# Column mean of an 8192 x 8192 matrix: plain two-row-group loads and three unsummed row groups left to TensorE

## The chip, the core and the metric

The kernel runs on one core of one Trainium2 chip. A core has TensorE (PE, matrix products), VectorE (DVE), ScalarE (ACT), GpSimd (POOL), SyncE (SP, here only an issuer of transfers) and 16 DMA engines that move data between the chip's memory and the core's own memory, SBUF. TensorE writes its results to a small accumulating memory, PSUM, from which ScalarE or VectorE must copy them before they can be stored. The metric is device time in microseconds (us) of one execution. SBUF has 128 partitions; a tile is written "partitions x elements".

## The reference

```python
def setup_inputs():
    return {"x": np.random.randn(8192, 8192).astype(np.float32)}

def reference(x):
    return np.mean(x, axis=0)
```

The input is 8192 rows of 8192 float32 numbers, 268.4 MB. The output is one row of 8192 numbers, the mean of each column. Every input byte is read once and takes part in one addition.

## The kernel before, in words

**Tiling.** The rows are cut into G = 64 row groups of 128 rows, one row for each partition; a group is 4 MB. The columns are counted in 16 blocks of F = 512, and W = 128 is a quarter of a block. The buffer `bufs` holds six whole row groups: slots 0 to 3 are a ring for loads, slot 4 is `both` (the sum of the two groups of a load), and slot 5 is `acc`, the running sum over row groups. VectorE adds row groups into `acc`, so that `acc` becomes 128 partial sums for each column. Summing over the 128 partitions is left to TensorE: a matmul with `ones` (128 x 32, every value 1/8192) as weights gives the sum over partitions. Each matmul makes 32 equal output rows, so four of them, at four column tiles of the array (`tile_position=(0, 32 * q)`), fill the 128 partitions of one PSUM tile with four different stretches of columns. A float32 matmul of the code is two MATMUL records in the profile.

**Loads.** All loads go out from SyncE in the order of the program (`load`, L73). A load waits for the add that last read its slot, and each second one also for two loads eight places back. First come 512 KB of row group 60 (blocks 14 and 15) into a separate tile `early`, then groups 0 to 3 as one load of 16 MB, groups 4 and 5 as one load, and 1.25 MB of group 63 (blocks 9 to 13) into `early`. After that groups 6 to 55 come two at a time (`load_rows`, L89), groups 56 to 59 one at a time, group 60 without the two blocks that came early, 61 and 62 whole, and the rest of group 63 in four pieces: blocks 4 to 7, 0 to 3, 14 to 15, and 8.

**VectorE.** `add` (L94) makes one addition. For a pair of groups there are two: `both` = first + second, then `acc` += `both`; the ring slot is free for the next load after the first of them. A no-op on ScalarE or GpSimd waits for the load and for the addition ahead together, and the addition waits for that no-op. Groups 56 to 60 are added to `acc` singly. Of group 60 only blocks 0 to 13 are added, of group 61 only blocks 7 to 15.

**GpSimd** adds the two early pieces into `acc` while VectorE and the loads go on (L129), and at the end three blocks of group 62 (L148).

**TensorE** runs 63 matmuls at the end, in the order of the list `sums` (L155 to L180): blocks of `acc` and of groups 61, 62 and 63, ordered by when each becomes final, into the PSUM tiles `bank0`, `bank1`, `wide`, `two` and `last`. The list is executed in that order, whatever is ready.

**Results.** ScalarE copies four of the PSUM tiles into the no longer used slot `both` (L198), VectorE copies `last` into `tail` (L214). Five stores (L201) go out, from SyncE and from ScalarE. SyncE then waits for every load and store, and the program ends.

The functions that the change touches:

Of the kernel before, what the change touches and what calls it, by code (L numbers as in the profile page):

```python
# [9 lines left out]
def kernel(  # L10
# [35 lines left out]
    sync = mybir.DependencyInfo(mybir.DependencyClass.Sync, mybir.DependencyReason.DATA)  # L46

    sb = ctx.enter_context(tc.tile_pool(name="sb", bufs=1))
    psp = ctx.enter_context(tc.tile_pool(name="psum", bufs=1, space=bass.MemoryType.PSUM))

    bufs = sb.tile([P, U, N], f32, name="bufs")
    both = bufs[:, U - 2, :]
    acc = bufs[:, U - 1, :]
    ones = sb.tile([P, 32], f32, name="ones")
    early = sb.tile([P, 7 * F], f32, name="early")
    tail = sb.tile([P, W], f32, name="tail")
    warm = sb.tile([P, 32], f32, name="warm")
    nc.gpsimd.memset(ones[:], 1.0 / M)  # L58
    ready = sb.tile([P, 1], f32, name="ready")
    tc.keep_in_program_order(  # L60
        nc.gpsimd.tensor_add(out=ready[:], in0=ones[:, 0:1], in1=ones[:, 1:2]))  # L61
    banks = [psp.tile([P, F], f32, name=f"bank{b}") for b in range(2)]
    wide = psp.tile([P, 2 * F], f32, name="wide")
    two = psp.tile([P, 2 * W], f32, name="two")
    last = psp.tile([P, W], f32, name="last")

    loads = []

    def landed(*inss):

        nop = tc.keep_in_program_order(nc.sync.nop()).ins
        for o in inss:
            tc.add_manual_dep(nop, o.name, sync, reason="SyncE waits")  # L73

    def load(dst, src):
        ins = tc.keep_in_program_order(nc.sync.dma_start(out=dst, in_=src)).ins  # L76
# [12 lines left out]
    def load_rows(g, u, n):  # L89
        return load(bufs[:, u:u + n, :], rows(g, n).rearrange("(p j) c -> p j c", j=n))  # L90

    adds, joins = [], {}

    def add(dst, a, b, dmas):  # L94

        ins = nc.vector.tensor_add(out=dst, in0=a, in1=b).ins  # L96
# [10 lines left out]
        tc.declare_no_dep(ins, group="early", reason="the no-op waited, or the add behind it")  # L107
        tc.add_to_no_dep_group("adds", ins)
        adds.append(ins)

    load(early[:, 5 * F:], rows(G - 4)[:, 14 * F:])
    first, second = load_rows(0, 0, 4), load_rows(4, 4, 2)
    load(early[:, :5 * F], rows(G - 1)[:, 9 * F:14 * F])
    add(bufs[:, 2:4, :], bufs[:, 2:4, :], bufs[:, 0:2, :], [first])
    add(bufs[:, 4:6, :], bufs[:, 4:6, :], bufs[:, 2:4, :], [second])
    add(acc, acc, both, [])
    tc.keep_in_program_order(nc.scalar.copy(out=warm[:], in_=ones[:]))  # L117
    ahead = []
    g = 6
    while g < G - 8:  # L120
        u = (g + 2) % 4
        dma = load_rows(g, u, 2)
        add(both, bufs[:, u, :], bufs[:, u + 1, :], [dma])
        add(acc, acc, both, ahead)
        ahead = []
        if g in (24, 32):
            lo, hi = (0, 4) if g == 24 else (4, 7)
            cols = slice((9 + lo) * F, (9 + hi) * F)
            ins = tc.keep_in_program_order(nc.gpsimd.tensor_add(  # L129
                out=acc[:, cols], in0=acc[:, cols], in1=early[:, lo * F:hi * F])).ins  # L130
            tc.add_to_no_dep_group("early", ins)
            ahead = [ins]
        g += 2

    while g < G - 4:
        row = bufs[:, (g + 2) % 4, :]
        add(acc, acc, row, [load(row, rows(g))])
        g += 1
    for lo, hi, loaded in [(0, 14, 14), (7, 16, 16)]:
        row = bufs[:, (g + 2) % 4, :]  # L140
        dma = load(row[:, :loaded * F], rows(g)[:, :loaded * F])
        cols = slice(lo * F, hi * F)
        add(acc[:, cols], acc[:, cols], row[:, cols], [dma])
        g += 1
    r61, r62, r63 = [bufs[:, (g + 1 + j) % 4, :] for j in range(3)]
    load(r62, rows(g))
    for cols in [slice(14 * F, 16 * F), slice(8 * F, 9 * F)]:
        joined = tc.keep_in_program_order(nc.gpsimd.tensor_add(  # L148
            out=acc[:, cols], in0=acc[:, cols], in1=r62[:, cols])).ins
    g += 1  # L150
    for lo, hi in [(4, 8), (0, 4), (14, 16), (8, 9)]:
        load(r63[:, lo * F:hi * F], rows(g)[:, lo * F:hi * F])

    sums = []

    def blocks(row, lo, hi):
        for i in range(lo, hi):
            sums.append((banks[i // 4], i % 4, 0, row[:, i * F:(i + 1) * F]))

    def spread(dst, row, lo, hi, part=slice(None)):  # L160
        n = (hi - lo) * W
        for c in range(0, n, F)[part]:
            for q in range(4):
                at = lo * F + q * n + c
                sums.append((dst, q, c, row[:, at:at + min(F, n - c)]))

    blocks(acc, 2, 5)
    blocks(acc, 0, 2)
    blocks(r61, 0, 7)
    blocks(acc, 5, 8)  # L170
    blocks(r62, 0, 8)
    spread(wide, acc, 9, 14, slice(1))
    blocks(r63, 4, 8)
    spread(wide, r62, 9, 14, slice(1))
    for row in (acc, r62):
        spread(wide, row, 9, 14, slice(1, 2))
    spread(two, acc, 14, 16)
    blocks(r63, 0, 4)
    spread(last, acc, 8, 9)
    spread(two, r63, 14, 16)  # L180
    spread(last, r63, 8, 9)
    for n, (dst, q, c, cols) in enumerate(sums):
        summed = tc.keep_in_program_order(nc.tensor.matmul(  # L183
            out=dst[32 * q:32 * q + 32, c:c + cols.shape[1]],
            lhsT=ones[:],
            rhs=cols,
            start=all((d is dst, k, at) != (True, q, c) for d, k, at, _ in sums[:n]),
            stop=all((d is dst, k, at) != (True, q, c) for d, k, at, _ in sums[n + 1:]),
            tile_position=(0, 32 * q),
            skip_group_check=True,  # L190
        )).ins

    res = both[:, :2 * F].rearrange("p (b c) -> p b c", b=2)
    res5 = both[:, 2 * F:2 * F + 5 * W]
    res2 = both[:, 4 * F:4 * F + 2 * W]

    def copy(dst, src):
        return tc.keep_in_program_order(nc.scalar.copy(out=dst, in_=src)).ins  # L198

    def store(engine, dst, src, *then):  # L200
        ins = tc.keep_in_program_order(engine.dma_start(out=dst, in_=src)).ins  # L201
        for o in then:
            tc.add_manual_dep(ins, o.name, sync, reason="follows that load")
        return ins

    def part(lo, hi):
        return out[lo * F:hi * F].rearrange("(q c) -> q c", q=4)

    copy(res[:, 1, :], banks[1][:])
    s1 = store(nc.scalar, part(4, 8), res[0:P:32, 1, :], loads[-4])  # L210
    copy(res5, wide[:, :5 * W])
    copy(res[:, 0, :], banks[0][:])
    copied = copy(res2, two[:])
    ended = nc.vector.tensor_copy(out=tail[:], in_=last[:]).ins  # L214
    landed(*joins.values())
    s5 = store(nc.sync, part(9, 14), res5[0:P:32, :], *loads[-7:-3])
    s0 = store(nc.sync, part(0, 4), res[0:P:32, 0, :])
    s2 = store(nc.scalar, part(14, 16), res2[0:P:32, :])
    store(nc.sync, part(8, 9), tail[0:P:32, :])
    landed(loads[-2], joined)  # L220
    landed(loads[-1], copied)
    landed(s0, s5)
    landed(s1, summed)
    landed(s2, ended)
# [32 lines left out]
```

## Time and profile before

| | |
|---|---|
| median of 3 runs | 628.5 us (628.38 to 628.59) |
| the profiled execution, first to last instruction (span) | 626.4 us |
| VectorE busy | 529.3 us, 85% of the span |
| TensorE busy | 13.3 us, 2%, all of it at the end |
| share of the 16 DMA engines' time taken by packets of the load queue | 99.3% |
| data rate over the span | 429 GB/s |

Of the profiled execution the page gives the span and not a total of its own; the median of the timed runs stands 2.1 us above that span, which is what lies around the first and last instruction. Where sums below are made, they are made inside the span, and the difference is put on the median.

The profile's views used here are the page itself (busy times, DMA queues, groups of instructions), the chain of waits (followed back from the last instruction: at each step what released it), and the timeline (instructions of each engine in order of time). In the chain, a piece named DMA is time in which the chain ran through a load. In the timeline PEld is the loading of weights for TensorE, PE the matmuls themselves; SPq and ACTq are the issuing of a transfer by SyncE or ScalarE.

### The profile page before, as it was taken

The numbers are of one execution on the slowest core, as the hardware profiler recorded it, in microseconds if no ns is written. First come the engines' busy times: TensorE is split into PE (matmuls) and PEld (weight loads), VectorE is DVE, ScalarE is ACT, GpSimd is POOL, SyncE is SP. The second block draws the span as 40 slices with busy tenths as digits, with TensorE's granted clock in tenths as the row PEclk, the third lists the DMA queues.
The fourth block names the chain that finished last, engine by engine and source line by source line (L and its number), as shares of the span: only waits on it lengthen the run. The fifth ranks groups of instructions, "written<-read, shape, count | busy, mean of one in ns | idle before, by whom it ended". The sixth has DMA issues, their size and how long they took to land.

```text
span 626.4 us, 484 instructions
## 1 busy us (share of the span) xinstructions
PE 13.3 (2%) x126; PEld 4.0 (1%) x126; DVE 529.3 (85%) x60; ACT 3.7 (1%) x6; POOL 12.0 (2%) x10
## 2 busy tenths in 40 slices
PE   0000000000000000000000000000000000000008
PEld 0000000000000000000000000000000000000002
DVE  0028999998888998889998899888898888999992
ACT  0000000000000000000000000000000000000001
POOL 0000000000000000020000200000000000000002
PEclk9999999999999999999999999999999999999999
DMA  8999999999999999999999999999999999999997
GB/s 372 465 402 428 459 410 460 402 469 402 469 402 469 402 469 402 469 402 469 402 465 406 439 431 427 444 410 460 402 469 402 469 402 469 402 435 435 419 435 305
DMA packets 5930, 268.50 MB, mean 429 GB/s; under 512 B 660, under 2 KB 668, under 8 KB 1064
## 3 DMA queue, kind: packets, MB, share of 16 engines
q1 hardware_dynamic: 5912, 268.46, 99.3%
q8 instruction: 1, 0.02, 0.0%
q10 hardware_dynamic: 16, 0.01, 0.0%
q14 instruction: 1, 0.01, 0.0%
HBM read 268.44 MB, written 0.03 MB: 429 GB/s over the span
## 4 chain that ended last, share of the span: by engine, by line
DMA 59%; DVE 30%; another core or an unknown queue 10%; issue 0%; SPq 0%; ACTq 0%; PE 0%; POOL 0%; POOLq 0%
DMA bufs<-in_x_dram 59%; DVE bufs L96 30%; SPq L76 0%; ACTq L99 0%; PE last L183 0%; DVE tail L214 0%; POOL ready L61 0%; POOL ones L58 0%; POOLq L99 0%; POOLq L241 0%
## 5 line engine op out<-in xcount | busy, mean ns | idle before, releaser
L96 DVE TENSOR_TENSOR bufs<-bufs 128x8192 f32<-128x8192 f32 (+3 forms) x59 | 529.0, 8966 | 85.9 <-DMA bufs<-in_x_dram 43.0
L183 PE MATMUL bank<-bufs,ones 128*32 128x512 f32 x62 | 10.0, 716 | 610.3 <-DVE bufs L96 610.0
L129 POOL TENSOR_TENSOR bufs<-bufs,early 128x2048 f32<-128x2048 f32 (+1 forms) x2 | 7.9, 3954 | 348.5 <-DVE bufs L96 348.5
L148 POOL TENSOR_TENSOR bufs<-bufs 128x1024 f32<-128x1024 f32 (+1 forms) x2 | 3.6, 1824 | 258.9 <-DMA bufs<-in_x_dram 258.9
L214 DVE COPY tail<-last 128x128 f32<-128x128 f32 x1 | 0.3, 291 | 8.8 <-PE last L183 8.8
L183 PEld LDWEIGHTS bank<-bufs,ones 128*32 128x32 f32 x62 | 2.2, 121 | 616.4 <-issue 614.5
L198 ACT COPY bufs<-bank 128x512 f32<-128x512 f32 x2 | 1.2, 586 | 617.9 <-PE bank L183 617.9
L183 PE MATMUL wide<-bufs,ones 128*32 128x512 f32 (+1 forms) x32 | 2.5, 432 | 0.0
L117 ACT ACT_TABLE_LOAD x1 | 1.3, 1283 | 0.7 <-PEq L241 0.7
L183 PE MATMUL two<-bufs,ones 128*32 128x256 f32 x16 | 1.2, 380 | 0.0
L183 PEld LDWEIGHTS wide<-bufs,ones 128*32 128x32 f32 x32 | 1.0, 110 | 1.8 <-issue 1.8
L183 PE MATMUL last<-bufs,ones 128*32 128x128 f32 x16 | 0.8, 279 | 0.1
L198 ACT COPY bufs<-wide 128x640 f32<-128x640 f32 x1 | 0.7, 692 | 1.1 <-PE wide L183 1.1
L183 PEld LDWEIGHTS last<-bufs,ones 128*32 128x32 f32 x16 | 0.4, 109 | 1.2 <-issue 0.6
L183 PEld LDWEIGHTS two<-bufs,ones 128*32 128x32 f32 x16 | 0.4, 109 | 0.1
L198 ACT COPY bufs<-two 128x256 f32<-128x256 f32 x1 | 0.4, 372 | 0.1
L117 ACT COPY warm<-ones 128x32 f32<-128x32 f32 x1 | 0.2, 217 | 0.0
L61 POOL TENSOR_TENSOR ready<-ones 128x1 f32<-128x1 f32 x1 | 0.2, 193 | 0.1
L58 POOL MEMSET ones<- 128x32 f32 x1 | 0.1, 125 | 0.3 <-POOLq L241 0.3
L241 POOL MEMSET const-float32-0.0<- 128x1 f32 x1 | 0.1, 98 | 0.2 <-issue 0.2
L241 POOL MEMSET const-bfloat16-1.0<- 128x1 bf16 x1 | 0.1, 102 | 0.0
L241 POOL MEMSET const-uint8-127<- 128x1 uint8 x1 | 0.1, 102 | 0.0
(1 smaller groups left out, 0.1 us busy)
## 6 DMA issues: line engine op xcount, KB each, us to landing
bufs<-in_x_dram SPq DMA_DIRECT2D x6, 4096.0 KB, 20.4
bufs<-in_x_dram SPq DMA_DIRECT2D x1, 3584.0 KB
bufs<-in_x_dram SPq DMA_DIRECT2D x2, 1024.0 KB, 18.7
early<-in_x_dram SPq DMA_DIRECT2D x1, 1280.0 KB
early<-in_x_dram SPq DMA_DIRECT2D x1, 512.0 KB
bufs<-in_x_dram SPq DMA_DIRECT2D x1, 512.0 KB, 19.4
bufs<-in_x_dram SPq DMA_DIRECT2D x27, 29.9
bufs<-in_x_dram SPq DMA_DIRECT2D x1, 256.0 KB, 19.7
```

What stands on the lines that cost most here:

```text
L58: nc.gpsimd.memset(ones[:], 1.0 / M)
L61: nc.gpsimd.tensor_add(out=ready[:], in0=ones[:, 0:1], in1=ones[:, 1:2]))
L96: ins = nc.vector.tensor_add(out=dst, in0=a, in1=b).ins
L117: tc.keep_in_program_order(nc.scalar.copy(out=warm[:], in_=ones[:]))
L129: ins = tc.keep_in_program_order(nc.gpsimd.tensor_add(out=acc[:, cols], in0=acc[:, cols], in1=early[:, lo * F:hi * F])).ins
L148: joined = tc.keep_in_program_order(nc.gpsimd.tensor_add(out=acc[:, cols], in0=acc[:, cols], in1=r62[:, cols])).ins
L183: summed = tc.keep_in_program_order(nc.tensor.matmul(out=dst[32 * q:32 * q + 32, c:c + cols.shape[1]], lhsT=ones[:], rhs=cols, start=all(( ...
L198: return tc.keep_in_program_order(nc.scalar.copy(out=dst, in_=src)).ins
L214: ended = nc.vector.tensor_copy(out=tail[:], in_=last[:]).ins
L241: nc = _bacc.Bacc("TRN2", target_bir_lowering=False, num_devices=1)
```

## The change

All loads but the last four now have two row groups each: 31 of them, for groups 0 to 61. The two early loads, the load of four groups, and the single loads are gone. Group 62 is one load; group 63 is three: blocks 0 to 10, 11 to 14, and 15.

VectorE makes 60 additions of a whole row group: one for groups 0 and 1 (straight into `acc`), two for each of the 29 pairs 2 to 59, and one for group 60. Groups 61, 62 and 63 are added by nobody; TensorE takes them whole. GpSimd adds nothing any more.

TensorE runs 80 matmuls: for each of `acc`, group 61, 62 and 63, in this order, the same 20 over all 16 blocks. The PSUM tiles are four banks (blocks 0 to 3, 4 to 7, 8 to 10, 11 to 14) and `last` (block 15).

The results get SBUF tiles of their own. ScalarE copies banks 0, 2 and 3, VectorE bank 1 and `last`. SyncE issues the stores of banks 0, 1, 2 and of `last`; ScalarE issues one, that of bank 3.

```diff
-    early = sb.tile([P, 7 * F], f32, name="early")
+    res = [sb.tile([P, w], f32, name=f"res{i}") for i, w in enumerate((F, F, 3 * W, F))]
...
-    load(early[:, 5 * F:], rows(G - 4)[:, 14 * F:])
-    first, second = load_rows(0, 0, 4), load_rows(4, 4, 2)
-    load(early[:, :5 * F], rows(G - 1)[:, 9 * F:14 * F])
-    add(bufs[:, 2:4, :], bufs[:, 2:4, :], bufs[:, 0:2, :], [first])
-    add(bufs[:, 4:6, :], bufs[:, 4:6, :], bufs[:, 2:4, :], [second])
-    add(acc, acc, both, [])
+    def pair(g):
+        u = g % 4
+        dma = load(bufs[:, u:u + 2, :], rows(g, 2).rearrange("(p j) c -> p j c", j=2))
+        return bufs[:, u, :], bufs[:, u + 1, :], dma
+
+    a, b, dma = pair(0)
+    add(acc, a, b, [dma])
...
-    while g < G - 8:
-        u = (g + 2) % 4
-        dma = load_rows(g, u, 2)
-        add(both, bufs[:, u, :], bufs[:, u + 1, :], [dma])
-        add(acc, acc, both, ahead)
...
-    while g < G - 4:
-        row = bufs[:, (g + 2) % 4, :]
-        add(acc, acc, row, [load(row, rows(g))])
-        g += 1
-    for lo, hi, loaded in [(0, 14, 14), (7, 16, 16)]:
...
-    for lo, hi in [(4, 8), (0, 4), (14, 16), (8, 9)]:
-        load(r63[:, lo * F:hi * F], rows(g)[:, lo * F:hi * F])
+    for g in range(2, G - 4, 2):
+        a, b, dma = pair(g)
+        add(both, a, b, [dma])
+        add(acc, acc, both, [])
+    a, r61, dma = pair(G - 4)
+    add(acc, acc, a, [dma])
+    r62, r63 = bufs[:, 2, :], bufs[:, 3, :]
+    load(r62, rows(G - 2))
+    for lo, hi in [(0, 11), (11, 15), (15, 16)]:
+        load(r63[:, lo * F:hi * F], rows(G - 1)[:, lo * F:hi * F])
...
-    blocks(acc, 2, 5)
-    blocks(acc, 0, 2)
-    blocks(r61, 0, 7)
-    blocks(acc, 5, 8)
-    blocks(r62, 0, 8)
-    spread(wide, acc, 9, 14, slice(1))
-    blocks(r63, 4, 8)
-    spread(wide, r62, 9, 14, slice(1))
-    for row in (acc, r62):
-        spread(wide, row, 9, 14, slice(1, 2))
-    spread(two, acc, 14, 16)
-    blocks(r63, 0, 4)
-    spread(last, acc, 8, 9)
-    spread(two, r63, 14, 16)
-    spread(last, r63, 8, 9)
+    for row in (acc, r61, r62, r63):
+        blocks(banks[0], row, 0)
+        blocks(banks[1], row, 4)
+        spread(banks[2], row, 8, 3)
+        blocks(banks[3], row, 11)
+        spread(last, row, 15, 1)
...
+    copy(0)
+    nc.vector.tensor_copy(out=res[1][:], in_=banks[1][:])
+    copy(2)
+    copied = copy(3)
...
+    s0 = store(nc.sync, 0, 4, res[0])
+    s4 = store(nc.sync, 4, 8, res[1])
+    s8 = store(nc.sync, 8, 11, res[2])
+    s11 = store(nc.scalar, 11, 15, res[3])
+    store(nc.sync, 15, 16, tail)
```

In the changed kernel `blocks(dst, row, lo)` adds four matmuls of 512 columns to the list, and `spread(dst, row, lo, n)` four matmuls of n times 128 columns.

More of the change, by code (lines that the diff above doesn't have):

```diff
@@ L61 @@
         nc.gpsimd.tensor_add(out=ready[:], in0=ones[:, 0:1], in1=ones[:, 1:2]))
-    banks = [psp.tile([P, F], f32, name=f"bank{b}") for b in range(2)]
-    wide = psp.tile([P, 2 * F], f32, name="wide")
-    two = psp.tile([P, 2 * W], f32, name="two")
+    banks = [psp.tile([P, w], f32, name=f"bank{b}") for b, w in enumerate((F, F, 3 * W, F))]
     last = psp.tile([P, W], f32, name="last")
@@ L87, in rows @@
         return x[g * P:(g + n) * P, :]
-    def load_rows(g, u, n):
-        return load(bufs[:, u:u + n, :], rows(g, n).rearrange("(p j) c -> p j c", j=n))
     adds, joins = [], {}
@@ L106, in add @@
             tc.declare_no_dep(ins, group="loads", reason="the add ahead waited")
-        tc.declare_no_dep(ins, group="early", reason="the no-op waited, or the add behind it")
         tc.add_to_no_dep_group("adds", ins)
         adds.append(ins)
-    load(early[:, 5 * F:], rows(G - 4)[:, 14 * F:])
-    first, second = load_rows(0, 0, 4), load_rows(4, 4, 2)
-    load(early[:, :5 * F], rows(G - 1)[:, 9 * F:14 * F])
-    add(bufs[:, 2:4, :], bufs[:, 2:4, :], bufs[:, 0:2, :], [first])
-    add(bufs[:, 4:6, :], bufs[:, 4:6, :], bufs[:, 2:4, :], [second])
@@ L116 @@
-    add(acc, acc, both, [])
-    tc.keep_in_program_order(nc.scalar.copy(out=warm[:], in_=ones[:]))
-    ahead = []
-    g = 6
-    while g < G - 8:
-        u = (g + 2) % 4
-        dma = load_rows(g, u, 2)
-        add(both, bufs[:, u, :], bufs[:, u + 1, :], [dma])
-        add(acc, acc, both, ahead)
[L125 to L133, printed above, removed]
@@ L135 @@
-    while g < G - 4:
-        row = bufs[:, (g + 2) % 4, :]
-        add(acc, acc, row, [load(row, rows(g))])
-        g += 1
-    for lo, hi, loaded in [(0, 14, 14), (7, 16, 16)]:
[L140 to L149, printed above, removed]
@@ L150 @@
-    g += 1
-    for lo, hi in [(4, 8), (0, 4), (14, 16), (8, 9)]:
-        load(r63[:, lo * F:hi * F], rows(g)[:, lo * F:hi * F])
-    sums = []
[L156 to L165, printed above, removed]
@@ L167 @@
-    blocks(acc, 2, 5)
-    blocks(acc, 0, 2)
-    blocks(r61, 0, 7)
-    blocks(acc, 5, 8)
-    blocks(r62, 0, 8)
-    spread(wide, acc, 9, 14, slice(1))
-    blocks(r63, 4, 8)
-    spread(wide, r62, 9, 14, slice(1))
-    for row in (acc, r62):
-        spread(wide, row, 9, 14, slice(1, 2))
-    spread(two, acc, 14, 16)
-    blocks(r63, 0, 4)
-    spread(last, acc, 8, 9)
-    spread(two, r63, 14, 16)
-    spread(last, r63, 8, 9)
-    for n, (dst, q, c, cols) in enumerate(sums):
+    def pair(g):
+        u = g % 4
+        dma = load(bufs[:, u:u + 2, :], rows(g, 2).rearrange("(p j) c -> p j c", j=2))
+        return bufs[:, u, :], bufs[:, u + 1, :], dma
@@ new lines, with blocks, spread @@
+    sums = []
+    def blocks(dst, row, lo):
+        for q in range(4):
+            sums.append((dst, q, row[:, (lo + q) * F:(lo + q + 1) * F]))
+    def spread(dst, row, lo, n):
+        for q in range(4):
+            at = lo * F + q * n * W
+            sums.append((dst, q, row[:, at:at + n * W]))
+    for row in (acc, r61, r62, r63):
[4 more added lines that the diff above has]
+        spread(last, row, 15, 1)
@@ L183 @@
+    for n, (dst, q, cols) in enumerate(sums):
         summed = tc.keep_in_program_order(nc.tensor.matmul(
-            out=dst[32 * q:32 * q + 32, c:c + cols.shape[1]],
+            out=dst[32 * q:32 * q + 32, :],
             lhsT=ones[:],
             rhs=cols,
-            start=all((d is dst, k, at) != (True, q, c) for d, k, at, _ in sums[:n]),
-            stop=all((d is dst, k, at) != (True, q, c) for d, k, at, _ in sums[n + 1:]),
+            start=all((d is dst, k) != (True, q) for d, k, _ in sums[:n]),
+            stop=all((d is dst, k) != (True, q) for d, k, _ in sums[n + 1:]),
@@ L191, with copy, store @@
         )).ins
[L193 to L213, printed above, removed]
+    def copy(i):
+        return tc.keep_in_program_order(nc.scalar.copy(out=res[i][:], in_=banks[i][:])).ins
+    def store(engine, lo, hi, src):
+        dst = out[lo * F:hi * F].rearrange("(q c) -> q c", q=4)
+        return tc.keep_in_program_order(engine.dma_start(out=dst, in_=src[0:P:32, :])).ins
+    copy(0)
+    nc.vector.tensor_copy(out=res[1][:], in_=banks[1][:])
+    copy(2)
+    copied = copy(3)
     ended = nc.vector.tensor_copy(out=tail[:], in_=last[:]).ins
     landed(*joins.values())
[L216 to L220, printed above, removed]
+    s0 = store(nc.sync, 0, 4, res[0])
[3 more added lines that the diff above has]
+    store(nc.sync, 15, 16, tail)
+    landed(loads[-2])
     landed(loads[-1], copied)
-    landed(s0, s5)
-    landed(s1, summed)
-    landed(s2, ended)
+    landed(s0, s4)
+    landed(s8, summed)
+    landed(s11, ended)
     hold = tc.keep_in_program_order(nc.vector.nop()).ins
```

## The prediction

> **What bounds the kernel now.** The page comes first: which resource is full.
>
> ```profile
> span 626.4 us, 484 instructions
> ...
> PE 13.3 (2%) x126; PEld 4.0 (1%) x126; DVE 529.3 (85%) x60; ACT 3.7 (1%) x6; POOL 12.0 (2%) x10
> ...
> q1 hardware_dynamic: 5912, 268.46, 99.3%
> ```
>
> The load queue keeps the 16 DMA engines busy for 99.3% of the span. VectorE is at 85%, so it follows the loads. Next the chain of waits, for the pace of the loads and for what lies behind the last one.
>
> ```profile
> 510.81 8.70 DVE bufs L96
> 519.53 29.92 DMA bufs<-in_x_dram
> ...
> 549.50 8.70 DVE bufs L96
> ...
> 603.45 19.74 DMA bufs<-in_x_dram
> 623.19 0.04 issue
> 623.23 0.47 PE last L183 x8
> ...
> 623.73 0.29 DVE tail L214
> ```
>
> The step from 510.81 to 549.50 is two pairs of row groups, 38.70 us, which makes 9.675 us for a group (4.19 MB, 433 GB/s). At the end the chain goes load, eight matmuls, one copy: TensorE is ready when the last load lands. That is the point to look at, since TensorE's list is what the change makes longer. Its pace stands in the timeline of PEld, whose pieces each open a batch of matmuls.
>
> ```profile
> 609.95 0.24 PEld L183 LDWEIGHTS bank<-bufs,ones 128*32 128x32 f32 x8 [609.95 <-issue]
> 610.85 0.18 PEld L183 LDWEIGHTS bank<-bufs,ones 128*32 128x32 f32 x1 [0.66 <-issue]
> 611.71 0.20 PEld L183 LDWEIGHTS bank<-bufs,ones 128*32 128x32 f32 x7 [0.68 <-issue]
> 612.56 0.18 PEld L183 LDWEIGHTS bank<-bufs,ones 128*32 128x32 f32 x1 [0.66 <-issue]
> 613.41 0.16 PEld L183 LDWEIGHTS bank<-bufs,ones 128*32 128x32 f32 x5 [0.68 <-issue]
> 613.88 0.12 PEld L183 LDWEIGHTS bank<-bufs,ones 128*32 128x32 f32 x3 [0.31 <-issue]
> ...
> 616.28 0.16 PEld L183 LDWEIGHTS bank<-bufs,ones 128*32 128x32 f32 x8 [1.19 <-DMA bufs<-in_x_dram]
> 616.73 0.13 PEld L183 LDWEIGHTS bank<-bufs,ones 128*32 128x32 f32 x4 [0.30 <-issue]
> 617.16 0.13 PEld L183 LDWEIGHTS bank<-bufs,ones 128*32 128x32 f32 x4 [0.30 <-issue]
> 617.59 0.13 PEld L183 LDWEIGHTS wide<-bufs,ones 128*32 128x32 f32 x4 [0.30 <-issue]
> ```
>
> A batch is four matmul records at the four column tiles, side by side. It takes 0.43 us for 512 columns (616.73, 617.16, 617.59), and 0.86 us in the first 3.4 us of the stage (610.85, 611.71, 612.56, 613.41): TensorE starts at half pace. A float32 matmul is two records (126 records, 63 matmuls in the code), so four matmuls of 512 columns, 2048 columns of a row group, cost two batches, 0.86 us, not 0.43. A whole row group of 8192 columns costs 8 batches, 3.45 us (the 384- and 128-column pieces go by their columns: eight records of 128 in `last` take 0.22 us, from 622.32 to 622.54).
>
> In the old list the waits for loads (1.19 us at 616.28, for one) show that TensorE had slack.
>
> **The change part by part.**
>
> *Start of the loads.* The small `early` load ahead of everything is gone; a pair comes first. In the windows of the first 4 us the 512 KB and the first 1 MB of large packets are all landed by 4.0 us, 1.57 MB, and nothing before 1.75. Taken as a fill time the small load may have cost up to 0.9 us more than its 1.2 us of bandwidth, or the same delay may fall on any first load (or 0.1 more for the longer issue, 0.47 against 0.39 us). Bounds -0.9 and +0.1; I take -0.3, nearer to the second, because a first-transfer delay is likelier than one of small pieces.
>
> *Pace of the loads.* A slot is free after the first add of its pair, 8.70 us plus about 0.5 after landing, while the other pair still needs 19.35 us: 10 us of cover. The 27 large loads show it: 29.9 us from issue to landing, 10.5 of them in the queue behind the one ahead. Cost nothing; without that cover, one bubble a pair.
>
> *VectorE.* 60 adds of 8.70 us, against 55 such, two of 17.23 and two partial ones. Two adds, 17.4 us, go by in the 19.35 us of a pair; cost nothing, and the earlier first add (pair 0 lands at some 23 us instead of 42.99) gains nothing, since each later add waits for its own load.
>
> *GpSimd's adds, early pieces.* They lengthened two adds (11.21 and 10.12 us in the chain, not 8.70), but the next load then came 2.5 us and 1.4 us sooner after the add. Nothing on the path.
>
> *When VectorE is done.* At 549.50 VectorE saw group 55: 56 groups and 7 early blocks, 56.44 groups, which puts the origin at 549.50 - 56.44 x 9.675 = 3.47. The pair of groups 60 and 61 is then seen at 3.47 + 62 x 9.675 = 603.3, and the last add, a whole group, ends at 612.0. Before, it was the last 9 blocks (4608 elements), which ended at 614.89 (549.50 + 65.39 for eight adds), but TensorE had begun at 609.98 on what was final. Now its list begins with `acc`, and group 61, there since 603.3, stands behind it.
>
> *TensorE.* The first matmul follows an add's end by 0.06 us (614.89 to 614.95): 612.1. Four rows of 8 batches are 32 x 0.432 = 13.8 us. The cold start adds four batches at 0.86 for 0.43: 1.7 us. End of the list: 612.1 + 13.8 + 1.7 = 627.6. Does it wait for loads? Group 62 would be seen at 3.47 + 63 x 9.675 = 613.0, needed at 612.1 + 1.7 + 2 x 3.45 = 620.7; group 63's last piece at about 622.7, needed from 624.1 on. It doesn't wait any more: the last load leaves the path, and TensorE takes its place.
>
> The cold start is bounded by none (-1.7) and by the whole list at half pace (+12.1). I take the row. The Trainium skill ("TensorE: Matmul & The Clock Gate", "What's actually happening") gives the rule that the array is throttled to half clock until about 3.4 us of sustained work, counted in a free-running window, so that the transition varies. The trace agrees with 3.4 us; by the rule's variation a whole window more could be cold, and the sum would be 1.7 us higher. The rule speaks against this change, which puts more work behind a cold start.
>
> *The end.* Before, the last eight records ended at 623.23 + 0.22 = 623.45, and the span 2.94 us later, through copy, store and final waits. The same stands behind the new list: 630.5. New is that bank 3, ScalarE's, is final only 0.22 us ahead of `last`: copy 0.59 us (the 128x512 row of L198), then the first transfer that ScalarE issues. Its two issues of before took these times:
>
> ```profile
> 620.60 1.07 ACTq L201 DMA_DIRECT2D out_dram<-bufs  x1
> ...
> 623.63 0.51 ACTq L201 DMA_DIRECT2D out_dram<-bufs  x1
> ...
> 624.04 0.50 SPq L201 DMA_DIRECT2D out_dram<-tail  x1
> ```
>
> With 0.51 it ends about when the `tail` store does (1.1 us behind the list; before, 624.54 - 623.45), with 1.07 it ends 0.6 later. Bounds 0 and +0.6; I take +0.6, since the longer row is ScalarE's first too: 631.1. SyncE's three stores ahead of `tail` (0.50 to 0.65 us each) fit: bank 1 is final 1.7 us before the list ends, and VectorE's copy of it, between 0.3 us (the 128-column row) and four times that, still leaves SyncE free within 0.1 us of the time when `tail` is ready.
>
> *Sum:* 631.1 - 0.3 = 630.8 against a span of 626.4: +4.4 us. On the median of 628.5 that is **632.9 us**, slower by 0.7%.
>
> **The rivals.**
>
> *TensorE stays hidden (not slower).* If the four rows took no more than 10.6 us (from 612.1 to the last landing, about 622.7), the load would still end last, and the time would be 628.5 - 0.3, plus up to 0.6 for ScalarE's store: 628.2 to 628.8. For it: TensorE is busy 2% of the span. Against it: 10.6 us for 32 batches needs 0.33 us each with no cold start, and no run of 512-column batches in the trace is below 0.43. 5 in 100.
>
> *The clock stays low for longer.* With one more window of 3.4 us at half pace, 634.6; with all of it, 645. For it: every row of before comes from one start, 609.98. Against: it sped up at 613.4 although VectorE and the loads were busy as they will be now. 10 in 100.
>
> *The loads get bubbles.* A slot freed later than 10 us after landing would stop the queue, 29 times. At 1 us each, 632.9 + 29 = 662. Against: the pairs from group 6 to 55 ran in the same ring at 19.35 us each with 99.3% busy. 3 in 100.
>
> *The sum as it stands*, with terms within their bounds: 82 in 100.
>
> **How the numbers follow.** About 0.2%, 1.3 us, is what a measurement of this kernel can tell from no change; the sum is more than three times that. The lower end takes the start gain to its bound (-0.6), ScalarE's store at 0.51 (-0.6) and 0.4 for a clock that rises sooner: 631.3. The upper takes a whole cold window (+1.7) and no gain at the start (+0.3): 634.9. Outside lie the hidden TensorE, the longer cold clock and the bubbles, under 2 in 10. Only the first rival is not slower: same 0.04, faster 0.01, slower 0.95.
>
> **What the changed profile would show.** Right: the chain's last pieces are PE and VectorE's last add of 8.70 us ending near 612, not a load; TensorE's batches run without a gap from 612 to about 627.6, at 0.86 and then 0.43; matmuls on group 62 and 63 name no DMA as releaser; the DMA slices fall to nothing from about 622.5, 8 us before the end; ScalarE's store takes about 1.07 us. Wrong: PE rows that still wait for DMA, a last load beyond 624, DMA idle between pairs, or batches of four at 0.22.

## The result, and the profile after

The changed kernel takes 634.56 us in the median (633.37 to 634.94), the kernel before, run beside it, 628.54 us: a ratio of 1.0094, 95% interval 1.008 to 1.0108. It is slower by 6.0 us; 4.4 us had been forecast. The profiled execution took 634.4 us, with a span of 632.6 us.

The page of the changed kernel, the lines that answer to those of before:

```profile
span 632.6 us, 530 instructions
...
PE 16.0 (3%) x160; PEld 5.7 (1%) x160; DVE 522.5 (83%) x62; ACT 3.2 (0%) x5; POOL 0.5 (0%) x6
...
q1 hardware_dynamic: 5072, 268.46, 98.3%
```

The loads still fill the span but for 1.7%, and TensorE is busy for 3% of it. Nothing in these shares says that TensorE is what the kernel waits for. The chain of waits of the changed kernel (start, length, what) says it:

```profile
574.20 29.92 DMA bufs<-in_x_dram
...
604.18 8.70 DVE bufs L67
612.88 0.14 issue
613.02 5.48 PE bank L118 x32
618.50 0.22 PE last L118 x8
618.72 3.22 PE bank L118 x32
621.94 0.22 PE last L118 x8
622.16 3.22 PE bank L118 x32
625.38 0.22 PE last L118 x8
625.60 3.26 PE bank L118 x32
628.86 0.02 issue
628.88 0.59 ACT res L129
```

Before, the chain's last long piece was a load that ended at 623.19. Now the last load in the chain is that of groups 60 and 61; VectorE's add of group 60 follows, and then the four rows of the list, `acc`, 61, 62 and 63, without a gap. Each row is 3.44 us, the first 5.70. The data of group 63 were all there by 623.2 in the packet records, 2.4 us before TensorE came to them.

The timeline of PEld in the changed kernel shows the pace of the first row:

```profile
612.99 0.23 PEld L118 LDWEIGHTS bank<-bufs,ones 128*32 128x32 f32 x8 [612.99 <-issue]
613.84 0.23 PEld L118 LDWEIGHTS bank<-bufs,ones 128*32 128x32 f32 x4 [0.62 <-issue]
...
616.40 0.23 PEld L118 LDWEIGHTS bank<-bufs,ones 128*32 128x32 f32 x4 [0.62 <-issue]
617.04 0.22 PEld L118 LDWEIGHTS bank<-bufs,ones 128*32 128x32 f32 x4 [0.41 <-issue]
617.45 0.14 PEld L118 LDWEIGHTS bank<-bufs,ones 128*32 128x32 f32 x4 [0.19 <-issue]
617.88 0.14 PEld L118 LDWEIGHTS last<-bufs,ones 128*32 128x32 f32 x4 [0.29 <-issue]
```

Batches of 0.86 us up to 616.40, then 0.64 for one of 384 columns, which is still half pace, and 0.43 from 617.45 on. The clock column of the profile's windows doesn't show the half pace. The windows of the changed kernel (for each engine busy time and instructions, then the granted clock, the DMA share and GB/s) have 1.00 in both of these stretches, and yet 20 matmul records in the one and 52 in the other:

```profile
613.00:617.00 4.00, 3.98 (x20) 1.14 (x24) 0.00 (x0) 0.00 (x0) 0.00 (x0) 1.00 1.05 451
617.50:621.50 4.00, 4.00 (x52) 1.53 (x48) 0.00 (x0) 0.00 (x0) 0.00 (x0) 1.00 0.90 378
```

The trace's own record of the granted clock, from which this column is made, begins only at 617.21 us here and at 613.47 in the kernel before, where the pace doubles; a stretch without a record reads 1.00. So the half pace lasted 4.2 us from the first matmul; before, 3.5.

Last, the end of the changed kernel, in the timeline of ScalarE, VectorE and the two issuing queues:

```profile
628.88 0.59 ACT L129 COPY res<-bank 128x512 f32<-128x512 f32 x1 [0.38 <-PE bank L118]
629.10 0.29 DVE L139 COPY tail<-last 128x128 f32<-128x128 f32 x1 [1.03 <-PE last L118]
629.42 0.51 SPq L133 DMA_DIRECT2D out_dram<-tail  x1
629.50 1.26 ACTq L133 DMA_DIRECT2D out_dram<-res  x1
```

ScalarE's store of bank 3 is the last to be issued. Before, ScalarE's last store was issued at 623.63 and the last of all was SyncE's, at 624.04.

### The profile page after: what moved, and what is told of

The parts are those of the page before. It is cut to its first block, busy times and chain, and to the rows that moved or that the text cites. A ratio compares the mean times of both kernels' runs of the same rounds, so it can differ in the third digit from the quotient of the medians.

```text
span 632.6 us, 530 instructions
## 1 busy us (share of the span) xinstructions
PE 16.0 (3%) x160; PEld 5.7 (1%) x160; DVE 522.5 (83%) x62; ACT 3.2 (0%) x5; POOL 0.5 (0%) x6
## 4 chain that ended last, share of the span: by engine, by line
DMA 75%; DVE 22%; PE 3%; issue 0%; ACT 0%; ACTq 0%
DMA bufs<-in_x_dram 75%; DVE bufs L67 22%; PE bank L118 2%; PE last L118 0%; ACT res L129 0%; ACTq L70 0%
## 5 line engine op out<-in xcount | busy, mean ns | idle before, releaser
L67 DVE TENSOR_TENSOR bufs<-bufs 128x8192 f32<-128x8192 f32 x60 | 521.5, 8692 | 91.3 <-ACTq L70 43.2
L118 PE MATMUL bank<-bufs,ones 128*32 128x512 f32 (+1 forms) x128 | 15.7, 638 | 613.0 <-DVE bufs L67 613.0
L118 PEld LDWEIGHTS bank<-bufs,ones 128*32 128x32 f32 x128 | 4.7, 122 | 620.7 <-issue 620.7
L129 ACT COPY res<-bank 128x512 f32<-128x512 f32 (+1 forms) x3 | 1.7, 550 | 625.6 <-PE bank L118 625.6
```

The costliest lines, as they stand in the source:

```text
L118: summed = tc.keep_in_program_order(nc.tensor.matmul(out=dst[32 * q:32 * q + 32, :], lhsT=ones[:], rhs=cols, start=all((d is dst, k) != (T ...
L129: return tc.keep_in_program_order(nc.scalar.copy(out=res[i][:], in_=banks[i][:])).ins
```

## The experiments

The theory: the end is set by a list of 80 matmuls that cannot begin before VectorE's last add ends, the first quarter of which runs at half pace. The rivals: the new loads made the end late and TensorE only follows; or it is the amount of TensorE's work that costs, whenever it begins. The kernel before, run beside each group of experiments, took 628.25 to 628.32 us in the median. Medians are of 4 to 11 executions, but for one kernel with a single one. Kernels called "from the changed kernel" are edits of it, the others edits of the kernel before.

**Group 61 first** (from the changed kernel).

```diff
-    for row in (acc, r61, r62, r63):
+    for row in (r61, acc, r62, r63):
```

> The changed kernel with one line altered: TensorE takes group 61 ahead of acc. Same loads, adds, matmuls and stores. Theory (the end is set by the 80 matmuls that begin only when the last add ends): group 61 (3.4 us, about 5.4 with the half-pace start) is done between 604.2 and 609.6, ahead of the end of the last add at 612.9; 60 matmuls, 10.3 us, are left. If the array keeps its pace through the gap of some 3.3 us, the list reaches 623.2 and the loads set the end again: about 629.5. If it falls back to half pace, the second start costs 1.9 again and the time is 634.5 - 3.4 = 631.1. Rival (the new load pattern made the end late, TensorE merely follows): no change, 634.5.

Measured: 630.19 us (630.11 to 630.55), 4.4 us less than the changed kernel with the same 80 matmuls; against the kernel before 1.0032 (1.002 to 1.0044). The timeline of TensorE (PE and PEld) in this kernel:

```profile
609.42 0.41 PE L118 MATMUL last<-bufs,ones 128*32 128x128 f32 x8
...
613.21 3.43 PE L118 MATMUL bank<-bufs,ones 128*32 128x512 f32 x32 [3.38 <-DVE bufs L67]
...
621.53 3.43 PE L118 MATMUL bank<-bufs,ones 128*32 128x512 f32 x32 [1.24 <-DMA bufs<-in_x_dram]
...
623.87 0.18 PEld L118 LDWEIGHTS bank<-bufs,ones 128*32 128x32 f32 x8 [0.47 <-DMA bufs<-in_x_dram]
624.17 0.48 ACT L129 COPY res<-bank 128x384 f32<-128x384 f32 x1 [0.92 <-PE bank L118]
624.48 0.13 PEld L118 LDWEIGHTS last<-bufs,ones 128*32 128x32 f32 x4 [0.43 <-DMA bufs<-in_x_dram]
```

The cold row is now that of group 61, done at 609.83 beside VectorE's last add. `acc` follows at 613.21 at full pace (3.43 us for the 32 records, not 5.48), and TensorE waits for loads again: 1.24 us for the first piece of group 63, and a little for each of the others. So the order of the list carries most of the change's cost. The rival "the loads are late" would have left the time at 634.5, and falls. The time is 0.7 us above the 629.5 expected. TensorE, idle for 3.38 us, started again at full pace in this execution, but not in all: two of the five have a mean granted clock of 0.997, which fits one fall to half pace for some 3.4 us, and the same list further down shows such a fall. Their times (630.19 and 630.27 us) are not longer, since the loads set the end.

**Group 60 to TensorE as well** (from the changed kernel), one add less for VectorE, 100 matmuls instead of 80.

```diff
-    a, r61, dma = pair(G - 4)
-    add(acc, acc, a, [dma])
+    r60, r61, dma = pair(G - 4)
...
-    for row in (acc, r61, r62, r63):
+    for row in (acc, r60, r61, r62, r63):
```

> The changed kernel without VectorE's last add: group 60 is left to TensorE too, order acc, 60, 61, 62, 63, 100 matmuls in place of 80 (TensorE works 3.4 us longer). Theory (what counts is when the list can begin): acc is final at 602.3, the list has 5.4 us for acc, then 3.4 us for each group, group 62 from 614.5, idle before the first piece of 63 at 620.5; the last load sets the end again: 628.5 to 629.5. Rival (the amount of TensorE's work is what costs): 634.5 + 3.4 = 637.9. Rival (load pattern): 634.5.

Measured: 630.1 us (630.07 to 631.58), 1.0035 (1.0022 to 1.0049). The timelines of TensorE, PE and then PEld:

```profile
602.80 6.02 PE L117 MATMUL bank<-bufs,ones 128*32 128x512 f32 x32 [602.80 <-DVE bufs L67]
...
621.01 3.53 PE L117 MATMUL bank<-bufs,ones 128*32 128x512 f32 x32 [1.66 <-DMA bufs<-in_x_dram]
```

```profile
623.47 0.16 PEld L117 LDWEIGHTS bank<-bufs,ones 128*32 128x32 f32 x8 [0.59 <-DMA bufs<-in_x_dram]
624.09 0.40 PEld L117 LDWEIGHTS last<-bufs,ones 128*32 128x32 f32 x8 [0.46 <-DMA bufs<-in_x_dram]
```

A quarter more matmuls, 3.4 us of work, and 4.5 us less time: `acc` is final one add and one landing sooner, the list begins at 602.80 and not at 613.02, and it ends with the loads. The amount of TensorE's work isn't what costs; its beginning is. This kernel too stays about 0.6 us above what was expected, nearly as much as the one above.

**TensorE kept busy ahead of the list** (from the changed kernel): 28 more matmuls on group 61 into a PSUM tile that nobody reads.

```diff
+    heat = psp.tile([P, F], f32, name="heat")
+    sums[:0] = [(heat, q, r61[:, (4 * k % 16 + q) * F:(4 * k % 16 + q + 1) * F])
+                for k in range(7) for q in range(4)]
```

> The changed kernel with 28 matmuls more ahead of the list, on group 61 into a PSUM tile that nobody reads, from its landing at 604.2 to about 612.2. Only the pace of TensorE at the start of the list changes. Theory: batches of 0.43 us from the first one on, 1.9 us saved on the 634.5: 632.6, with less spread between runs if the spread of 1.6 us comes from the half-pace start. Rival (the half pace at the start belongs to the first matmuls after the add, not to a cold array): no change, 634.5.

Measured: 631.98 us (631.95 to 632.12), 2.6 us less than the changed kernel; 1.006 (1.0047 to 1.0073). The timeline of TensorE, PE and then PEld:

```profile
603.95 7.57 PE L120 MATMUL heat<-bufs,ones 128*32 128x512 f32 x56 [603.95 <-DMA bufs<-in_x_dram]
612.62 3.43 PE L120 MATMUL bank<-bufs,ones 128*32 128x512 f32 x32 [1.10 <-DVE bufs L67]
```

```profile
613.07 0.13 PEld L120 LDWEIGHTS bank<-bufs,ones 128*32 128x32 f32 x4 [0.30 <-issue]
613.50 0.13 PEld L120 LDWEIGHTS bank<-bufs,ones 128*32 128x32 f32 x4 [0.30 <-issue]
```

The list runs from 612.62 to 626.40 in batches of 0.43 from its first, 13.8 us, as priced without the cold start; work that computes nothing made the kernel faster. The cold start inside the changed kernel's list was worth 2.05 us (15.84 - 13.78); the rest of the 2.5 us between the two profiled spans (632.6 and 630.1) is that the list follows the add by 0.04 us instead of 0.14, and an add that came 0.3 us sooner. The times lie within 0.17 us of each other, those of the changed kernel within 1.6, so most of what varies between executions there seems to go with the cold start. One execution of the kernel with group 60 is 1.5 us above its others (631.58 us); it is the one with a mean clock of 0.997.

**ScalarE's first store early** (from the changed kernel): the store of bank 0 moves from SyncE to ScalarE, so that bank 3's is ScalarE's second.

```diff
     copy(0)
+    s0 = store(nc.scalar, 0, 4, res[0])
...
-    s0 = store(nc.sync, 0, 4, res[0])
```

> The changed kernel with the store of bank 0 issued by ScalarE, right behind its copy, and not by SyncE. So ScalarE's first transfer falls 1.7 us before the end of the list, and its store of bank 3 is its second. Theory (the 1.26 us of the store of bank 3 are a cost of ScalarE's first transfer): the first issue takes 1.1 to 1.3 us, the last one 0.5, and the time falls by 0.7 to 633.8. Rival (the length comes with this store, for instance because SyncE issues at the same moment): the last issue stays near 1.2 us, time 634.5.

Measured: 634.47 us (633.56 to 634.93), 1.0094 (1.0079 to 1.011), the same as the changed kernel. The timeline of ScalarE's and SyncE's issues:

```profile
627.64 1.07 ACTq L133 DMA_DIRECT2D out_dram<-res  x1
...
629.39 0.58 ACT L129 COPY res<-bank 128x512 f32<-128x512 f32 x1 [0.16 <-PE bank L118]
...
629.95 0.50 SPq L133 DMA_DIRECT2D out_dram<-tail  x1
630.00 0.51 ACTq L133 DMA_DIRECT2D out_dram<-res  x1
```

The long issue is indeed the engine's first, 1.07 us, and the second is 0.51. But it buys nothing. SyncE's wait for this store ends 1.99 us after the issue begins (630.00 to 631.99); in the changed kernel, with an issue of 1.26 us, it ends after 1.97 (629.50 to 631.46). The length of the issue is not on the path. The fence also shows what is: the copy of bank 3 starts at 629.39, when the list is over, not 0.22 us ahead of that.

**No early loads, the rest as before** (from the kernel before): group 60 and group 63 are loaded whole in their places, GpSimd's two early adds are gone, and group 63's five blocks go into the list.

```diff
-    load(early[:, 5 * F:], rows(G - 4)[:, 14 * F:])
     first, second = load_rows(0, 0, 4), load_rows(4, 4, 2)
-    load(early[:, :5 * F], rows(G - 1)[:, 9 * F:14 * F])
...
-    for lo, hi, loaded in [(0, 14, 14), (7, 16, 16)]:
+    for lo, hi, loaded in [(0, 16, 16), (7, 16, 16)]:
...
-    for lo, hi in [(4, 8), (0, 4), (14, 16), (8, 9)]:
+    for lo, hi in [(4, 8), (9, 14), (0, 4), (14, 16), (8, 9)]:
...
+    spread(wide, r63, 9, 14, slice(1))
-    for row in (acc, r62):
+    for row in (acc, r62, r63):
```

> The kernel before without its two early loads: group 60 is loaded and added whole, blocks 9 to 13 of group 63 are a fifth piece at the end (second of the five) and 8 more matmuls of TensorE, GpSimd's two early adds are gone. First load, single loads and order of the list stay. So only this part of the change is made. Theory (the list of TensorE sets the end once it is later or longer): the add of group 60 takes 8.70 in place of 7.63 us, so the list begins 1.1 us later, and it is 1.1 us longer; before, it had waits of 1.8 us in it, so 0.4 to 1.0 us come out at the end: 629.0 to 629.4. Rival (early loads pay by the pace of the loads alone): no change, 628.4.

Measured: 631.07 us (630.62 to 631.34), 1.0043 (1.003 to 1.0057), 2 us more than expected. The loss is at 61 us, far from TensorE. The load of groups 6 and 7 needs the slots that the first add of two groups reads; that add ends at 59.33 and the load is issued behind it. By the packet records the load ahead, of groups 4 and 5, ended on the 16 engines at 60.48 to 61.06, and the first packets of the new one began at 60.74 to 62.68. The queue ran dry. The last packet of groups 6 and 7 ended at 82.90, 21.84 us after that of groups 4 and 5, where a pair takes 19.35: 2.5 us lost. The windows of this kernel and then of the next, for two row groups' time (the last three columns are the clock, the DMA share and GB/s; a packet's bytes count where it begins):

```profile
61.30:80.60 19.30, 0.00 (x0) 0.00 (x0) 19.09 (x2) 0.00 (x0) 0.00 (x0) 1.00 0.94 401
```

```profile
61.30:80.60 19.30, 0.00 (x0) 0.00 (x0) 17.39 (x2) 0.00 (x0) 0.00 (x0) 1.00 1.00 435
```

So in the kernel before, the 1.25 MB of group 63 behind the second load were also a cover for this add. Removed alone, they leave a hole; the change removes them together with the load of four groups that needed the cover.

**Pairs from the start, no early loads, list and end as before** (the kernel above, with one edit more): the front of the change alone.

```diff
-    first, second = load_rows(0, 0, 4), load_rows(4, 4, 2)
-    add(bufs[:, 2:4, :], bufs[:, 2:4, :], bufs[:, 0:2, :], [first])
-    add(bufs[:, 4:6, :], bufs[:, 4:6, :], bufs[:, 2:4, :], [second])
-    add(acc, acc, both, [])
+    first = load_rows(0, 2, 2)
+    add(acc, bufs[:, 2, :], bufs[:, 3, :], [first])
...
-    g = 6
+    g = 2
```

> The kernel before with loads of two groups from the first one on and without the early loads; its own end stays (single loads of groups 56 to 62, five pieces of group 63, the old list with 8 matmuls more). It is the front of the change alone. The experiment that took out the early loads and kept the load of four groups drained the load queue at 61 us and lost 2.5 us there. Theory (the early loads were cover for the large first load; with pairs the ring needs none): every load queued 10 us ahead, no gap at 61 us, VectorE's last adds and TensorE's list not later than before, the last load sets the end: 628.3 to 628.9, and 0.7 more if VectorE's instruction transfer falls within the loads. Rival (the early loads are worth 2.75 us by themselves): 631.

Measured: 629.05 us (628.82 to 629.71), 1.0013 (1.0004 to 1.0022): 0.8 us above the kernel before. So the front of the change costs little. TensorE is not what it waits for: the list begins sooner than before (609.95 there), and its last piece waits 0.49 us for a load (before, 0.55), at 623.72 and not at 623.23. One step of two pairs in VectorE's adds, from 429.00 to 468.31, is 39.31 us long and not 38.70; what lies there is looked at further down. The timeline of PEld:

```profile
607.22 0.24 PEld L172 LDWEIGHTS bank<-bufs,ones 128*32 128x32 f32 x8 [607.22 <-issue]
...
623.72 0.16 PEld L172 LDWEIGHTS last<-bufs,ones 128*32 128x32 f32 x8 [0.49 <-DMA bufs<-in_x_dram]
```

**A large load first** (from the kernel before): the 512 KB of `early` go behind the load of four groups. This tests the gain of 0.3 us at the start of the loads by itself.

```diff
-    load(early[:, 5 * F:], rows(G - 4)[:, 14 * F:])
-    first, second = load_rows(0, 0, 4), load_rows(4, 4, 2)
+    first = load_rows(0, 0, 4)
+    load(early[:, 5 * F:], rows(G - 4)[:, 14 * F:])
+    second = load_rows(4, 4, 2)
```

> The kernel before with its first two loads exchanged: the load of four groups goes first, the early load of 512 KB second. Same bytes, same everything behind. It asks what the first load of large packets costs at the start. In the changed kernel the first packets of 64 KB took 2.7 to 3.5 us and the last of the 16 engines ended its first at 5.5 us, against 6.36 us in the kernel before, which had 1.2 us more of data by then: 0.4 us lost. If this belongs to large packets first: landings 0.3 to 0.5 us later all along, time 628.8. If not: no change, 628.4.

Measured: 628.37 us (628.33 to 628.69), 1.0001 (0.9992 to 1.0009). The first adds of the kernel before and then of this one:

```profile
42.99 17.23 DVE L96 TENSOR_TENSOR bufs<-bufs 128x16384 f32<-128x16384 f32 x1 [42.99 <-DMA bufs<-in_x_dram]
```

```profile
42.11 17.22 DVE L96 TENSOR_TENSOR bufs<-bufs 128x16384 f32<-128x16384 f32 x1 [42.11 <-DMA bufs<-in_x_dram]
```

The kernel before is 0.88 us later with 1.21 us more of data, so the small load first puts it 0.33 us ahead. By the add of groups 10 and 11 the two stand together (123.78 and 123.81): the lead is gone again, and the time is the same. Small packets ahead of all cost nothing in the end, and the gain of 0.3 us from leaving them out isn't there.

**Where VectorE's instructions are fetched.** The packet records of the changed kernel hold a transfer of 8 KB on a queue named "instruction" at 462.4 us, in the middle of the loads; it takes 0.33 us on one of the 16 DMA engines, and the 64 KB load packet behind it takes 3.08 us instead of 2.42. So that engine falls back by 0.98 us against the others (0.33 for the transfer and 0.66 for the longer packet; the texts put on record ahead of these runs count only the 0.66), and stays there. Another engine was 0.42 us late already, so the load landed 0.55 us later, and not 0.98. The chain of the changed kernel has it, beside a load of the usual length:

```profile
418.82 29.93 DMA bufs<-in_x_dram
...
457.52 30.48 DMA bufs<-in_x_dram
```

The kernel before has this transfer only at 626.0, behind the loads. If it belongs to VectorE's list of instructions, eight instructions more at the start of VectorE's work must bring it eight adds forward, to 462.4 - 8 x 9.675 = 385 us (from the changed kernel):

```diff
     a, b, dma = pair(0)
+    for k in range(8):
+        tc.keep_in_program_order(nc.vector.tensor_copy(out=tail[:, k:k + 1], in_=ones[:, 0:1]))
```

> The changed kernel with eight copies of one column by VectorE ahead of its first add, under 1 us in all and long done when the first load lands. It asks whose instructions the transfer of 8 KB at 462 us is, that held up one DMA engine's packet by 0.66 us in the changed kernel and in the four experiments. If VectorE's: it comes eight adds, four pairs, 77 us earlier, near 385 us. If SyncE's or another's: it stays at 462 us. The time stays at 634.5 in both.

And sixty such copies, beside group 61 first, should take it ahead of nearly all the loads:

> The kernel with group 61 first in the list (630.2) and 60 one-column copies by VectorE ahead of its first add, some 6 us of its 22 us of idle time. The 8 KB instruction transfer of VectorE, at the issue of about its 46th instruction, so comes in the first 10 us and not at 462 us, where it held up one DMA engine by 0.66 us. Theory (that delay stands to the end, since every load waits for its slowest engine, and the loads set this kernel's end): if the transfer falls into the uneven start of the 16 engines and is absorbed there, 629.5; if the engine that carries it is among the late ones already, the delay only moves and the time stays at 630.2. Rival (the delay is made up later): 630.2, and the spread between the engines at the last landings is the same 1.1 to 1.6 us without any long packet after the start.

Where the transfer stands in the packet records, and the times:

```
kernel                           8 KB instruction transfer   time, us
before                           626.0 us, behind the loads  628.54
changed                          462.4                       634.56
changed, 8 copies                384.8                       634.21 (one run)
pairs from the start             462.0                       629.05
group 61 first                   462.7                       630.19
group 61 first, 60 copies          7.4                       630.20
```

It came at 384.8: it is VectorE's stream. (The traces that hold 67 instructions of VectorE have the transfer only behind the loads; those of the changed kernel and of pairs from the start hold 69 and have it at 462.) But with sixty copies the time was 630.2 us (630.07 to 630.47), 1.0032 (1.002 to 1.0043), as without them. The transfer met a load packet at 7.4 us (2.95 us for it), and the DMA engines stood 1.0 us apart from 22.78 us, when the first pair had landed, to 603.27, when the last had. The lateness of one engine is only moved, not absorbed; a load is there when its last engine is. So these runs show whose transfer it is and that its place within the loads makes no difference. What the kernel would take without it within the loads has no run.

The profile of this last kernel also shows a fall of the clock, which the one of group 61 first doesn't have. The list is the same, and TensorE, idle for only 2.55 us, took up `acc` at half pace: 4.99 us for the 32 records and not 3.43, with a granted clock of 0.50.

```profile
612.57 4.99 PE L120 MATMUL bank<-bufs,ones 128*32 128x512 f32 x32 [2.55 <-DVE bufs L67]
```

```profile
612.40:615.70 3.30, 3.13 (x16) 0.79 (x20) 0.12 (x1) 0.00 (x0) 0.00 (x0) 0.50 1.02 437
```

## Why the prediction was right or wrong

The direction, the mechanism and most of the terms were right: TensorE takes the place of the last load, and the median lies within the range, 1.7 us above the number. That it stays within is in part luck: the upper end was set by a whole window more at half pace, which did not come, and most of that room was filled by what the prediction didn't have. The terms, against the profiled execution:

| step | predicted | measured |
|---|---|---|
| last add begins | 603.0 (603.3, less 0.3 at the start) | 604.18 |
| last add takes | 8.70 | 8.70 |
| first matmul behind it | 0.06 | 0.14 |
| list | 15.5 (13.8 + 1.7) | 15.84 |
| from there to the end of the span | 3.5 | 3.74 |
| span | 630.8 | 632.6 |

*Start of the loads* was mis-sized: the changed kernel's first add is at 22.81, which puts the origin of its loads' line at 22.81 - 2 x 9.675 = 3.46, the 3.47 that the prediction set out from. So the term is 0 and not -0.3, and the large load first made no difference to the time of the kernel before either. The bound of -0.9 came from a misreading: the windows count a packet's bytes where it begins. The 16 packets of 64 KB that began by 3.94 us ended at 5.87 to 6.36, so 1.57 MB had not landed at 4.0.

*Pace of the loads* was right in its mechanism. The pairs come every 38.70 us for two, as before (565.48 to 604.18), and no bubbles appear. The "10 us of cover" hold for pairs of a ring; the kernel without early loads shows what happens without cover, 2.5 us for one dry moment.

*When VectorE is done* was mis-sized by 1.2 us, the largest miss. The origin of the loads' line is 604.18 - 62 x 9.675 = 4.33, not 3.47. Of the 1.2 us, 0.3 are the gain at the start that doesn't exist, and 0.55 the fetch of VectorE's instructions, which the prediction didn't have at all: the change gives VectorE two more instructions, and one fetch that fell behind the loads now falls among them. Another 0.2 are one load, issued at 186.41, that took 30.12 us in the chain and not 29.93; why is open.

*GpSimd* and *VectorE's instruction count* at nothing: right as times of the engines. What the edit of VectorE's adds did cost was a transfer, not time of VectorE.

*TensorE*: 13.8 us for the list is right to 0.1 (13.78 in the kernel that starts warm). The cold start, 1.7 taken, was 2.05. "Half pace for 3.4 us" was one value of a quantity that varies. From the first matmul to the beginning of the clock's record, half pace lasted 2.8 us in the kernel with unread matmuls, 3.4 with group 61 first, 3.5 before, 4.2 in the changed kernel, 5.3 with group 60 on TensorE and 5.5 with ScalarE's store early. The record says more. In all eleven traces every stretch between two changes of the clock is a whole multiple of 3.41 us (3.41, 13.65, 17.07, 20.48, 23.89), so here the clock changed only on such a beat. How long a list is cold would then depend on where on the beat it begins: one beat at half pace costs 1.7 us, as an estimate of what can differ between executions, and the changed kernel's four lie within 1.6. The rival "one more window" (+1.7, 634.6 us) bounds this, and its time is the one that was measured, but not for its reason: of the miss of 1.8 us the clock has 0.35. The Trainium skill ("TensorE: Matmul & The Clock Gate", "What you observe") puts the transition at around 4 us, give or take 500 ns; these traces, one execution of each kernel, spread from 2.8 to 5.5, so here its spread is too narrow.

*The end* had nearly the right size for a wrong reason. 0.6 us was put on the length of ScalarE's first issue, and the run with an issue of 0.51 us took the same time. What is there instead: the copy of bank 3 begins only when the whole list ends, so ScalarE's store is issued 0.64 us behind it (629.50; before, 623.63, 0.18 behind 623.45), and SyncE's wait for it ends 1.97 us after that, against 1.62 for the smaller last store of before. 0.46 + 0.35 makes the 0.8 us by which 3.74 is more than 2.94. Why the copy doesn't start when bank 3's last matmul ends, and why the store of 8 KB takes 0.35 us longer than that of 4 KB, is open.

*The rivals.* "TensorE stays hidden" is out: it ended 5.7 us after the last packet of the loads. It is nearly true, at 630.1 to 630.2 us, when the list begins with a row that is final. "Bubbles" didn't occur.

**Where the 6.0 us went.** By differences of medians: 4.4 us is the list behind the last add with its cold start (group 61 first takes it away; 4.1 when each of the two is taken against the kernel before that ran beside it, 6.0 and 1.9), 0.8 the front of the change (pairs from the start, by itself), and some 0.8 the end, by the profile alone. These needn't add exactly, since each was measured in another company. What group 61 first leaves above the kernel before, 1.9 us, is made of the last two and of about 0.3 more. In its last loads the DMA engines stand 1.6 us apart, 1.1 before a fetch of 16 KB of instructions that falls among them at 619.3 us; in the changed kernel it falls at 622.17. It also comes sooner with group 60 on TensorE (614.5) and with the unread matmuls (617.2), which would fit a fetch of TensorE's own; that was not tested.

No kernel tried here beats the one before.

## What to carry to other kernels

An engine that runs a list in order should begin with what is final first: here the first of four rows was the one that became final last, and swapping two names in a tuple gave back some 4 of 6.0 us. A share of busy time of 3% says nothing about an engine whose work all lies at the end; price its list from batches of the trace, from the moment its first operand is final, with a cold start on top, and let it run on data that are there (or on anything) ahead of the critical part. Before removing a small load or a partial add that looks like an ornament, look for what its time covers: the queue at 61 us ran dry without it.

## What the runs showed of the hardware that was not expected

- TensorE's half pace at the start of a list lasted 2.8 to 5.5 us in six kernels, and the granted clock in the profile's windows reads 1.00 all through it. The spacing of the batches shows it, and the place where the trace's record of the clock begins.
- Full pace outlasted an idle gap of 3.38 us (group 61 first) and of 1.10 us (the unread matmuls) in the profiled executions, but not one of 2.55 us (group 61 first with sixty copies). So the length of the gap alone doesn't tell.
- The fetch of an engine's instructions can delay loads: 8 KB in 0.33 us set one DMA engine back by 0.98 us and one load's landing by 0.55 us, and nothing absorbed it in the 140 us that followed. The Trainium skill ("Runtime: NRT & Kernel Launch", "Instruction fetch mechanics") calls the cost of going from one block of instructions to the next mostly hidden. It is hidden from the engine that runs the instructions, which here shows no gap of its own; it isn't from loads that keep all 16 DMA engines full.
- An issue of a store on ScalarE took 1.07 to 1.26 us the first time and 0.51 the second, but SyncE's wait for the store ended 1.97 and 1.99 us after the issue began in either case.
